# Memory attention: the rests of all key, value and query weights by VectorE, and the query weight sums loaded later

## The chip, the cores and the metric

One core of a Trainium2 chip runs the whole layer. The metric is device time of one execution in microseconds (us). Its engines are TensorE (PE, with its weight loads as PEld), VectorE (DVE), ScalarE (ACT), GpSimd (POOL) and SyncE (SP). SP and POOL issue the DMA transfers of this part; 16 DMA engines of the core carry them.

## The reference

A decoder layer for 512 positions of width 1024: a SwiGLU half-step, token mixing, memory cross-attention, a second SwiGLU half-step, a final norm. The change lies in the cross-attention, which is

```python
def memory_xattn(h, m, w_xq, w_xkv, w_xo):
    q = (h @ w_xq).reshape(B, S, XATTN_HEADS, XATTN_HEAD_DIM) * XATTN_HEAD_DIM ** -0.5
    k, v = jnp.split(m @ w_xkv, 2, axis=-1)
    p = jax.nn.softmax(jnp.einsum('bshd,bmhd->bhsm', q, k).astype(jnp.float32), axis=-1)
    o = jnp.einsum('bhsm,bmhd->bshd', p.astype(v.dtype), v)
    return o.reshape(B, S, D_MODEL) @ w_xo
```

with 256 rows of memory `m`, 4 heads of width 256, and `h` and `m` normed before. Inputs are float32.

## The kernel before

Every float32 operand of a product is kept as two rounded parts: a high part (ScalarE's rounded copy) and the rest (VectorE's `raw - high`). A product is three matmuls: high by high, high by rest, rest by high. `split` (L114, L115) makes the two parts.

The cross-attention first makes keys and values in 16 steps, `for i in range(NKV)`: steps 0 to 7 are the column blocks of the key weights (`in_w_xk_dram`, 24 matmuls of 256 columns each, into `ps_d`), steps 8 to 15 the blocks of the value weights (`in_w_xv_dram`, 12 matmuls of 512 columns each, into two banks `ps_s` for 8 to 11 and two banks `ps_t` for 12 to 15). Each step uses one 512 KB block. It is loaded by SP into one of three buffers `wr` (`fetch`), and `cut` makes its parts: three blocks ahead of the loop, blocks 3 and 4 in step 0, then block i+4 in step i, until block 15 in step 11. So a block is cut four steps before it is used. `cut` ends with the `fetch` of the block that is three further on, which takes the buffer that the cut frees. The parts go into `w` (two halves of 512 columns, blocks in `LOOSE`), `xqh`/`xql` or `wh`/`wl`.

Inside the loop every engine runs its instructions in the order in which the code issues them (`ordered`). In step i come: the cut, the matmuls, the evacuation of the step before (`evacuate`: `kh`, `kl`, and the two `vh`, `vl` behind steps 11 and 15), the calls on query weights, and then one or two pieces of `work`: the normed input as sums of quarters for the query product, made by VectorE with some ScalarE (`yt`, `xph`, `w3h`, `xpl`, `K`, `nh`, `nl`).

For the blocks in `SHARED` the rest isn't made by VectorE. In `added`, ScalarE copies the block twice, once as it is and once negated, and a POOL transfer adds the block from HBM once more to the negated copy.

The query product of a head uses sums of weight blocks, in `xs` (`s` in the code, two buffers): `load_q` has SP load one block twice, `add_q` has POOL add two other halves to it by an adding transfer. `load_r` and `load_r2` load the blocks `r1` (in a `wr` buffer) and `r2`. In steps 12 and 13 the parts of head 0's weights `w1` and `w2` are made. Then `heads(0)` to `heads(3)` follow: `heads(hd)` makes head hd's query in seven products, and in it the sums and parts of head hd+1's weights (`e["s"]`, `e["w1"]`, `e["w2"]`).

Of the kernel before, what the change touches and what calls it, by code (L numbers as in the profile page):

```python
# [71 lines left out]
def hybrid_layer(ctx: ExitStack, tc: tile.TileContext, a: dict):  # L72
# [16 lines left out]
    @contextmanager  # L89
    def ordered():  # L90
        Engine.pinned = True
        yield
        Engine.pinned = False
# [19 lines left out]
    def split(h, l, src):  # L113
        A.activation(h, src, AF.Copy)  # L114
        V.tensor_sub(l, src, f32(h))  # L115

    def wpair():
        return (g.tile([P, 1024], F32R, tag="wh", name="wh", bufs=2),
                g.tile([P, 1024], F32R, tag="wl", name="wl", bufs=2))
# [811 lines left out]
    with tc.tile_pool(name="mix", bufs=1, reuse_waits="tile") as mp:  # L931
# [121 lines left out]
        for c in range(4):  # L1053
            h, l = wload(a["vcat"][:, c * 2 * VC:(c + 1) * 2 * VC], 2 * VC)
            for kk in range(2):
                k = 2 * c + kk
                w = slice(kk * VC, (kk + 1) * VC)
# [385 lines left out]
    with tc.tile_pool(name="xa", bufs=1, reuse_waits="tile") as xp:  # L1443
# [11 lines left out]
        def part(hl, src, j):  # L1455
            split(*hl, src[:, j * 512:j * 512 + 512])
# [4 lines left out]
        kv = [a["w_xk"][m] for m in range(KT)] + [a["w_xv"][f, c] for f in range(2) for c in range(4)]  # L1461
        NKV = len(kv)
        raws, cuts = [], []
        SHARED = (7, 9, 11, 13)
        LOOSE = (0, 1, 2, 7, 8, 9, 12, 13, 14)

        def fetch():
# [5 lines left out]
        def share(i, h, l, c):  # L1473
            if i not in SHARED:
                return split(h, l, raws[i][:, c])
            added(h, l, raws[i][:, c], kv[i][:, c])

        def added(h, l, raw, src):

            A.activation(h, raw, AF.Copy)  # L1480
            A.activation(l, raw, AF.Copy, scale=-1.0)
            G.dma_start(l, src, accum_op=ALU.add)

        def cut():
            i = len(cuts)
            if i in LOOSE:
                cuts.append([[big(F32R, "w0") for _ in range(2)] for _ in range(2)])
                for j in range(2):
                    share(i, cuts[i][0][j], cuts[i][1][j], slice(j * S, j * S + S))
            else:  # L1490
                cuts.append(wpair() if i in (5, 6) else qpair())
                share(i, *cuts[i], slice(0, 1024))
            fetch()
# [6 lines left out]
        def memory(i):  # L1500
            h, l = cuts[i]
            if i < KT:
                pk[i] = bank("d")
                for k in range(KT):
                    for z, (w, m) in enumerate(((h, gh[k]), (h, gl[k]), (l, gh[k]))):
                        w = w[k // 4][:, k % 4 * P:][:, :P] if i in LOOSE else w[:, k * P:(k + 1) * P]
                        T.matmul(pk[i][:, :MEM], w, m, start=k + z == 0, stop=k == KT - 1 and z == 2)
                return
            c = i % 4
            pk[i] = [bank("st"[i // 4 - 2]) for _ in range(MT)] if c == 0 else pk[i - 1]  # L1510
            for kk in range(2):
                k = 2 * c + kk
                w = slice(kk * 512, kk * 512 + 512)
                for t in range(MT):
                    tk = slice(t * P, (t + 1) * P)
                    for z, (m, ww) in enumerate(((gh, h), (gh, l), (gl, h))):
                        T.matmul(pk[i][t], m[k][:, tk], ww[kk] if i in LOOSE else ww[:, w], start=k + z == 0,
                                 stop=k == KT - 1 and z == 2)

        def evacuate(i):  # L1520
            if i < KT:
                split(kh[i], kl[i], pk[i][:, :MEM])
            elif i % 4 == 3:
                for t in range(MT):
                    split(vh[t][i // 4 - 2], vl[t][i // 4 - 2], pk[i][t])
# [3 lines left out]
        def load_q(hd):  # L1529
            w1 = a["w_xq"][2 * hd + 1]  # L1530
            xw[hd]["s"] = xp.tile([P, 1536], F32, tag="S", name="xs3", bufs=2)
            t = xw[hd]["s"][:, 512:].rearrange("p (j c) -> p j c", j=2)
            SY.dma_start(t, bass.AP(w1.tensor, w1.offset, [[1024, P], [0, 2], [1, 512]]))

        def add_q(hd):
            w0 = a["w_xq"][2 * hd]
            t = xw[hd]["s"][:, 512:].rearrange("p (j c) -> p j c", j=2)
            G.dma_start(t, bass.AP(w0.tensor, w0.offset, [[1024, P], [P * 1024 + 512, 2], [1, 512]]),
                        accum_op=ALU.add)

        def load_r(hd):
            xw[hd]["r1"] = raw_tile()
            SY.dma_start(xw[hd]["r1"], a["w_xq"][2 * hd])

        def load_r2(hd):
            d = xw[hd]
            d["r2"] = xp.tile([P, 1024], F32, tag="R2", name="r2", bufs=1)
            SY.dma_start(d["r2"][:, :512], a["w_xq"][2 * hd + 1][:, 512:])
# [55 lines left out]
        with ordered():  # L1604
            for i in range(NKV):
                for _ in range(1 if i else 2):
                    if len(cuts) < NKV:
                        cut()
                    elif len(cuts) == NKV and "r1" not in xw[0]:
                        load_r(0)  # L1610
                        load_r2(0)
                        load_r(1)
                        load_r(2)
                memory(i)
                if i == 0:
                    st = n3.sums()
                    n3.r = n3.rstd(st, NT)
                elif i == 1:
                    n3.spread()
                if i:  # L1620
                    evacuate(i - 1)
                if i in (0, 2):
                    load_q(i // 2)
                elif i in (3, 5):
                    add_q(i // 5)
                if i == NKV - 4:
                    d = xw[0]
                    d["w2"], w = wpair(), wpair()
                    d["w1"] = [[t[:, c:c + 512] for t in w] for c in (0, 512)]
                    added(*w, d["r1"], a["w_xq"][0])  # L1630
                    part([t[:, 512:] for t in d["w2"]], d["s"], 1)
                elif i == NKV - 3:
                    V.tensor_add(d["s"][:, :512], d["s"][:, 1024:], d["r1"][:, :512])
                    part([t[:, :512] for t in d["w2"]], d["s"], 0)
                for _ in range(0 if i < 2 else 1 if i < 9 else 2):
                    if work:
                        work.pop(0)()
            while work:
                work.pop(0)()
            evacuate(NKV - 1)  # L1640
# [274 lines left out]
```

## Time and profile before

| what | us |
|---|---|
| median of 3 runs (lowest, highest) | 1245.64 (1244.54, 1246.74) |
| profiled execution | 1245.68 |
| its span, first to last instruction | 1243.9 |
| PE busy | 1226.9 (99%) |
| DVE busy | 992.9 (80%) |
| ACT busy | 754.0 (61%) |
| POOL busy | 97.3 (8%) |

The span starts at 0; all times below count from there. A matmul that overlaps the next is counted as busy to its modelled end, so 99% doesn't mean that PE runs at its best pace: a wait shows as idle time before an instruction, a low clock as a longer distance from one matmul's start to the next. The granted clock is 1.00 at full speed. The DMA share is the busy share of the 16 engines; it can come out a little over 1.

### The profile page before, as it was taken

The numbers are of one execution on the slowest core, as the hardware profiler recorded it, in microseconds if no ns is written. First come the engines' busy times: TensorE is split into PE (matmuls) and PEld (weight loads), VectorE is DVE, ScalarE is ACT, GpSimd is POOL, SyncE is SP. The second block draws the span as 40 slices with busy tenths as digits, with TensorE's granted clock in tenths as the row PEclk, the third lists the DMA queues.
The fourth block names the chain that finished last, engine by engine and source line by source line (L and its number), as shares of the span: only waits on it lengthen the run. The fifth ranks groups of instructions, "written<-read, shape, count | busy, mean of one in ns | idle before, by whom it ended". The sixth has DMA issues, their size and how long they took to land.

```text
span 1243.9 us, 19322 instructions
## 1 busy us (share of the span) xinstructions
PE 1226.9 (99%) x7113; PEld 1070.2 (86%) x7113; DVE 992.9 (80%) x2018; ACT 754.0 (61%) x1506; POOL 97.3 (8%) x123
## 2 busy tenths in 40 slices
PE   9999999999999999999999997999999999999997
PEld 7888888879989788888887896997888888888997
DVE  5899888888787978787778667775698888889774
ACT  5466666556555777776874456664456666655553
POOL 0001110221110000000001011000001111100000
PEclk9999999999999999999999999999999999999999
DMA  6737775688544522222234377332456777727441
GB/s 223 186 109 194 187 190 149 188 254 246 138 150 129 168 67 84 81 67 77 68 102 169 102 230 202 102 94 68 111 152 169 188 184 196 178 87 207 134 134 69
DMA packets 64944, 181.38 MB, mean 146 GB/s; under 512 B 6616, under 2 KB 6896, under 8 KB 64848
## 3 DMA queue, kind: packets, MB, share of 16 engines
q1 hardware_dynamic: 45920, 132.70, 32.4%
q0 software_dynamic: 18496, 46.63, 18.3%
q8 instruction: 56, 0.92, 0.3%
q10 hardware_dynamic: 432, 0.81, 0.2%
q14 instruction: 40, 0.33, 0.1%
HBM read 175.87 MB, written 10.07 MB: 149 GB/s over the span
## 4 chain that ended last, share of the span: by engine, by line
PE 92%; DVE 3%; DMA 2%; ACT 1%; issue 1%; DVEq 0%; SPq 0%; POOL 0%; ACTq 0%; POOLq 0%
PE ps_d L139 30%; PE ps_d L87 21%; PE ps_t L87 13%; PE ps_s L87 7%; PE ps_o L87 6%; PE ps_d L1313 4%; PE ps_d L614 2%; PE ps_t L1198 1%; PE ps_s L1111 1%; PE ps_o L1106 1%; PE ps_s L1110 1%; PE ps_o L1105 1%; DMA xql<-in_w_xv_dram 1%; DMA xs<-in_w_xq_dram 1%; PE ps_d L1061 1%
## 5 line engine op out<-in xcount | busy, mean ns | idle before, releaser
L114 ACT ACTIVATE wh<-wr 128x512 fp32r<-128x512 f32 (+2 forms) x158 | 105.0, 695 | 100.7 <-issue 44.6
L139 PE MATMUL ps_d<-xh,wl 128*128 128x512 f32 x360 | 144.6, 402 | 0.1
L139 PE MATMUL ps_d<-xh,wh 128*128 128x512 f32 x360 | 143.3, 398 | 0.0
L139 PE MATMUL ps_d<-xl,wh 128*128 128x512 f32 x360 | 143.2, 398 | 0.0
L115 DVE TENSOR_TENSOR wl<-wr,wh 128x512 fp32r<-128x512 f32 (+2 forms) x158 | 119.0, 775 | 22.7 <-ACT wh L114 20.7
L87 DVE TENSOR_TENSOR wl<-wr,wh 128x1024 fp32r<-128x1024 f32 (+2 forms) x73 | 76.9, 1058 | 25.9 <-ACT wh L87 25.7
L139 PEld LDWEIGHTS ps_d<-xh,wl 128*128 128x128 f32 x360 | 67.8, 188 | 13.8 <-DVE wl L115 0.5
L139 PEld LDWEIGHTS ps_d<-xl,wh 128*128 128x128 f32 x360 | 67.8, 188 | 13.1
L87 ACT ACTIVATE wh<-wr 128x1024 fp32r<-128x1024 f32 (+2 forms) x74 | 67.9, 923 | 18.3 <-PE ps_o L87 4.6
L139 PEld LDWEIGHTS ps_d<-xh,wh 128*128 128x128 f32 x360 | 67.9, 189 | 12.9
L87 PE MATMUL ps_d<-b,wh 128*128 128x512 f32 (+1 forms) x220 | 64.0, 350 | 0.0
L87 DVE TENSOR_TENSOR s<-s,wr 128x512 f32<-128x512 f32 (+1 forms) x84 | 63.9, 760 | 0.0
L87 DVE TENSOR_TENSOR h2l<-s,h2h 128x512 fp32r<-128x512 f32 x68 | 44.1, 688 | 8.4 <-ACT h2h L87 8.1
L87 PE MATMUL ps_o<-t,h2h 128*128 128x256 f32 x272 | 50.4, 283 | 0.0
L87 PE MATMUL ps_d<-n,h2h 128*128 128x512 f32 x136 | 49.9, 401 | 0.1
L87 PE MATMUL ps_d<-b,wl 128*128 128x256 f32 x178 | 49.9, 280 | 0.0
L87 PE MATMUL ps_d<-t,h4h 128*128 128x512 f32 x136 | 49.6, 399 | 0.0
L87 PE MATMUL ps_t<-b,h5h 128*128 128x512 f32 x136 | 49.4, 397 | 0.0
L87 PE MATMUL ps_t<-n,h3h 128*128 128x512 f32 x136 | 49.3, 395 | 0.0
L87 PE MATMUL ps_s<-b,wh 128*128 128x512 f32 x136 | 49.1, 395 | 0.0
L1093 ACT ACTIVATE pth<-ps_t 128x512 fp32r<-128x512 f32 (+1 forms) x64 | 32.6, 524 | 18.7 <-PE ps_t L1198 15.5
L87 ACT ACTIVATE h2h<-s 128x512 fp32r<-128x512 f32 x68 | 39.1, 623 | 7.6 <-DVE s L87 7.6
(567 smaller groups left out, 3906.5 us busy)
## 6 DMA issues: line engine op xcount, KB each, us to landing
wr<-in_w_in_dram SPq DMA_DIRECT2D x29, 512.0 KB, 3.6
wr<-in_w_gate_dram SPq DMA_DIRECT2D x25, 512.0 KB, 5.1
wr<-in_w_up_dram SPq DMA_DIRECT2D x25, 512.0 KB, 5.3
wr<-in_w_down_dram SPq DMA_DIRECT2D x24, 448.0 KB, 3.5
s<-in_w_gate_dram SPq DMA_DIRECT2D x17, 512.0 KB, 4.5
s<-in_w_gate_dram POOLq DMA_DIRECT2D x17, 512.0 KB, 6.0
s<-in_w_up_dram SPq DMA_DIRECT2D x17, 512.0 KB, 4.3
s<-in_w_up_dram POOLq DMA_DIRECT2D x17, 512.0 KB, 6.4
```

Source lines behind the costliest of these rows:

```text
L87: return lambda *args, **kw: tc.keep_in_program_order(call(*args, **kw))
L114: A.activation(h, src, AF.Copy)
L115: V.tensor_sub(l, src, f32(h))
L139: yield T.matmul(out, w[:, c], m, start=i == 0, stop=i == total - 1)
L614: T.matmul(two[m], w[:, cc], v, start=f == 0 and z == 0, stop=f == NA - 1 and z == 2)
L1061: T.matmul(pv[i][:, :VC], m[k][:, tk], ww[:, w], start=k == 0 and z == 0, stop=k == KT - 1 and z == 2)
L1093: A.activation(h[:, :n], pt[:, :n], AF.Copy)
L1105: T.matmul(po[:, cols], w, h[:, src], start=start, stop=False, skip_group_check=True)
L1106: T.matmul(po[:, cols], w, l[:, src], start=False, stop=False, skip_group_check=True)
L1110: first = T.matmul(out, q[:, tk], kk[0][:, ks], start=True, stop=False)
L1111: T.matmul(out, q[:, tk], kk[1][:, ks], start=False, stop=True)
L1313: yield T.matmul(pj, w[:, c], m, start=n == 0, stop=n == 11)
```

## The change

`SHARED` becomes empty, so that all 16 blocks are split by ScalarE and VectorE, and the same holds for head 0's `w1`, whose two halves are split in steps 12 and 14. `load_q` of heads 0 and 1 moves from steps 0 and 2 to steps 6 and 12, `add_q` from steps 3 and 5 to steps 8 and 14.

```diff
-        SHARED = (7, 9, 11, 13)
+        SHARED = ()
...
-                if i in (0, 2):
-                    load_q(i // 2)
-                elif i in (3, 5):
-                    add_q(i // 5)
+                if i in (6, 12):
+                    load_q(i // 12)
+                elif i in (8, 14):
+                    add_q(i // 14)
                 if i == NKV - 4:
...
-                    added(*w, d["r1"], a["w_xq"][0])
+                    part(d["w1"][0], d["r1"], 0)
                     part([t[:, 512:] for t in d["w2"]], d["s"], 1)
+                elif i == NKV - 2:
+                    part(d["w1"][1], d["r1"], 1)
                 elif i == NKV - 3:
```

On POOL eight adding transfers go (two halves each for blocks 7, 9 and 13, one whole for block 11, one whole for head 0's `w1`); only the four of the query sums are left. On ACT the negated copies go.

VectorE in step 3, where block 7 is cut (`w` its parts, `wr` the raw block; the rows around it are the first `work` and the rest of the keys of step 2):

```order
 L87 SCALAR_TENSOR_TENSOR xph<-x_7583,gains,rb 128x512
+L87 TENSOR_TENSOR w_8152<-wr,w_8150 128x512
+L87 TENSOR_TENSOR w_8153<-wr,w_8151 128x512
 L87 TENSOR_TENSOR kl<-ps_d,kh 128x256
 L87 TENSOR_TENSOR w3h<-yt 128x256
```

Two subtractions stand now ahead of the evacuation and of the work of that step; blocks 9, 11 and 13 get theirs in the same way (11 as one of 1024 columns).

VectorE from step 12 on (`xs_8073` and `xs_8311` are the sums of head 0, `wl` the rests of its weights, `nl` and `vl` rests of sums of the input and of values):

```order
 L87 TENSOR_TENSOR vl<-ps_s,vh 128x512 x2
-L87 TENSOR_TENSOR wl<-xs_8073,wh 128x512
+L87 TENSOR_TENSOR wl<-wr,wh 128x512
+L87 TENSOR_TENSOR wl<-xs_8311,wh 128x512
 L87 TENSOR_TENSOR nl<-xpl,nh 128x512 x2
-L87 TENSOR_TENSOR xs_8073<-xs_8073,wr 128x512
-L87 TENSOR_TENSOR wl<-xs_8073,wh 128x512
+L87 TENSOR_TENSOR xs_8311<-xs_8311,wr 128x512
+L87 TENSOR_TENSOR wl<-xs_8311,wh 128x512
 L87 TENSOR_TENSOR nl<-w3l,nh 128x512
```

One subtraction for `w1` is new here, and one more stands two rows further down, behind the first rest `nl<-xph`.

SP from the loads of the last key blocks on (`xs_8073` and `xs_8148` are the sums of heads 0 and 1 before, `xs_8311` and `xs_8506` the same now):

```order
 L87 DMA wr<-in_w_xk_dram 128x1024 x2
-L87 DMA xs_8073<-in_w_xq_dram 128x2x512
+L87 DMA wr<-in_w_xv_dram 128x1024 x6
+L87 DMA xs_8311<-in_w_xq_dram 128x2x512
 L87 DMA wr<-in_w_xv_dram 128x1024 x2
-L87 DMA xs_8148<-in_w_xq_dram 128x2x512
-L87 DMA wr<-in_w_xv_dram 128x1024 x6
 L87 DMA wr<-in_w_xq_dram 128x1024
```

The load for head 0 moved behind six value blocks. The load for head 1, not in this piece, stands now behind all value blocks and behind the three loads of `r1`.

## Rows read from the trace of the kernel before

**Rows 1.** Busy us (and instructions) per engine, clock, DMA share, GB/s by stretch:

```profile
core 0: us, PE busy (x) PEld busy (x) DVE busy (x) ACT busy (x) POOL busy (x), PEclk, DMA share, GB/s
721.30:745.91 24.61, 24.61 (x209) 24.61 (x208) 15.69 (x29) 14.58 (x27) 5.88 (x6) 1.00 0.80 227
745.91:765.75 19.84, 13.48 (x51) 9.93 (x50) 16.15 (x33) 11.36 (x20) 2.60 (x3) 0.91 1.06 286
765.75:776.74 10.99, 10.99 (x49) 9.01 (x48) 7.23 (x12) 7.78 (x13) 0.84 (x1) 1.00 0.34 68
```

**Rows 2.** PE in order of time: start, us, what, [idle before <- releaser]:

```profile
750.71 0.50 PE L87 MATMUL ps_s<-w,gh 128*128 128x512 f32 x1 [1.66 <-DMA w<-in_w_xv_dram]
...
753.32 0.50 PE L87 MATMUL ps_s<-w,gh 128*128 128x512 f32 x1 [0.95 <-DMA w<-in_w_xv_dram]
...
761.52 0.50 PE L87 MATMUL ps_s<-xql,gh 128*128 128x512 f32 x1 [3.74 <-DMA xql<-in_w_xv_dram]
...
763.25 0.63 PE L87 MATMUL ps_s<-xqh,gh 128*128 128x512 f32 x1
763.68 0.63 PE L87 MATMUL ps_s<-xql,gh 128*128 128x512 f32 x1
...
786.73 1.59 PE L87 MATMUL ps_d<-K,w 128*128 128x256 f32 x12
```

**Rows 3.** The chain that ended last, 715 to 800: start, us, what:

```profile
732.50 9.04 DMA xs<-in_w_xq_dram
...
749.29 12.19 DMA xql<-in_w_xv_dram
```

**Rows 4.** DMA issues from 738 to 745: KB each, median us to landing:

```profile
w<-in_w_xv_dram POOLq DMA_DIRECT2D x2, 256.0 KB, 11.9
...
xs<-in_w_xq_dram POOLq DMA_DIRECT2D x1, 512.0 KB, 16.4
```

**Rows 5.** DMA issues of the whole execution:

```profile
wr<-in_w_out_dram SPq DMA_DIRECT2D x8, 512.0 KB, 3.6
wr<-in_w_xk_dram SPq DMA_DIRECT2D x8, 512.0 KB, 3.8
wr<-in_w_xv_dram SPq DMA_DIRECT2D x8, 512.0 KB, 7.8
...
xs<-in_w_xq_dram SPq DMA_DIRECT2D x4, 512.0 KB, 5.2
...
wl<-in_w_xq_dram POOLq DMA_DIRECT2D x1, 512.0 KB, 5.3
```

**Rows 6.** DVE in order of time:

```profile
732.34 0.74 DVE L87 SCALAR_TENSOR_TENSOR yt<-x,gains,rb 128x512 f32<-128x512 f32 x1
733.00 0.74 DVE L87 SCALAR_TENSOR_TENSOR xph<-x,gains,rb 128x512 f32<-128x512 f32 x1
733.84 0.42 DVE L87 TENSOR_TENSOR kl<-ps_d,kh 128x256 fp32r<-128x256 f32 x1
734.18 0.41 DVE L87 TENSOR_TENSOR w3h<-yt 128x256 f32<-128x256 f32 x1
...
735.98 1.29 DVE L87 TENSOR_TENSOR w<-wr,w 128x512 fp32r<-128x512 f32 x2
737.18 0.42 DVE L87 TENSOR_TENSOR kl<-ps_d,kh 128x256 fp32r<-128x256 f32 x1
...
782.60 1.23 DVE L87 TENSOR_TENSOR wl<-r,wh 128x1024 fp32r<-128x1024 f32 x1 [2.00 <-ACT wh L87]
...
784.42 0.68 DVE L87 TENSOR_TENSOR xs<-xs,wr 128x512 f32<-128x512 f32 x1
785.02 0.68 DVE L87 TENSOR_TENSOR w<-wr,w 128x512 fp32r<-128x512 f32 x1
```

**Rows 7.** DVE from 721 to 777 by shape: busy us, mean ns, idle before:

```profile
L87 DVE TENSOR_TENSOR kl<-ps_d,kh 128x256 fp32r<-128x256 f32 x8 | 3.4, 421 | 4.2 <-ACT kh L87 4.1
```

**Rows 8.** ACT from 721 to 777 by shape:

```profile
L87 ACT ACTIVATE wh<-wr 128x1024 fp32r<-128x1024 f32 x3 | 3.2, 1051 | 0.0
```

## The prediction

> **What bounds the kernel now.** The shares of busy time come first: PE is busy nearly all the time, so whatever an edit gains has to come out of PE's own waits. The chain that ended last, followed through the cross-attention, leaves PE in one place only for long: it goes through two transfers, the load of a query sum (9.04 us) and the adding transfer of value block 11 (12.19 us) [rows 3]. PE in order of time shows what the chain costs there: three waits in steps 9 and 11, of 1.66, 0.95 and 3.74 us, 6.35 us together, each for an added rest, and behind the longest one matmuls that start 0.43 us apart [rows 2]. The same kind of matmul in steps 12 to 15 needs 10.99 us for 48, so 0.229 us each, at a granted clock of 1.00 [rows 1]. 0.43 us is about twice that, which is the 1.2 GHz level instead of 2.4, after an idle time of PE.
>
> The table by stretch gives the whole loss without counting single matmuls. Steps 8 to 11 and steps 12 to 15 have the same 48 matmuls of 512 columns. The first four take 19.84 us, the last four 10.99 us [rows 1]. The loss is 19.84 - 10.99 = 8.85 us: 6.35 us of idle time and 2.50 us of low clock. In the first stretch the DMA share is 1.06 at 286 GB/s, in the last it is 0.34 [rows 1]; steps 0 to 7 ran at 1.00 clock without a PE wait, but with a DMA share of 0.80 already. So the bound of steps 8 to 11 is transfers. What waits are the adds, 9 to 16 us from issue to landing there [rows 3, 4], while the last add, issued when the engines had little else to do, landed in 5.3 us [rows 5].
>
> **What is removed.** Between steps 3 and 11 four blocks, 4 x 512 KB, are no longer fetched a second time, and these fetches were the only ones for which PE waited. The two query sums (2 x 2 transfers of 512 KB) leave the start of the loop. Left are the plain loads, 512 KB per step, and in the middle the sum of head 0. A step needs 2.75 us of PE (10.99 / 4), so the plain stream is 524 KB / 2.75 us = 191 GB/s, an estimate that leaves a third of the 286 GB/s seen free. Loads at such a pace landed in 3.6 us (the output weights of the stage before) and 3.8 us (key weights) [rows 5]. The three waits go for certain, since no matmul reads an added rest any more; what may be late instead is the subtraction that replaces it. With no wait in place of these the gain is the whole 8.85 us. ScalarE loses its negated copies and is far from full (11.36 of 19.84 us [rows 1]); I cost that at nothing.
>
> **What is added, on VectorE.** A rest of 1024 columns in two halves takes 1.20 us from start to start (735.98 to 737.18), a key rest 0.34 us (733.84 to 734.18), the two scalings of one `work` 1.32 us (2 x 0.66, from 732.34 and 733.00 on, so through at 733.66), the five sums 1.80 us (734.18 to 735.98) [rows 6]; 512 columns are half of 1.20, 0.60 us. Four more blocks are 4.8 us, the two halves of `w1` 1.2 us: 6.0 us more work in the loop. Is there room? I lay VectorE's instructions out in their new order from 733.66 us on, where the trace of before stops to hold: 9 blocks (7 to 15) 10.80, 6 key rests 2.04, 3 scalings 3.96, 4 groups of sums 7.20, 12 rests of input sums 7.20, 2 value rests 1.20, 4 halves of head 0's weights 2.40, one addition 0.60, and one wait of about 0.6 for ScalarE in step 13, where the high part of the sum just made has to come first. That is 36.0 us, so VectorE would be through at 769.7. PE, without waits from 745.91 on, ends step 15 at 745.91 + 96 x 0.229 = 767.9. VectorE is thus full from step 3 on, and behind at the end.
>
> It does no harm as long as each piece is in time. By this layout block 13 is cut at 751.5 and used from 759.6, block 15 at 759.5 and used from 765.1: the cuts are 5 to 8 us early, since a block is cut four steps ahead. At the end head 0's query needs the rest of `r2` (`wl`), in its sixth product. Before, it was done at 783.83, 7.1 us after PE left step 15 at 776.74, and had waited 2.00 us for ScalarE, which hung on PE [rows 6]. Now it would come 1.2 (value rests) + 0.6 (`w3`) + 0.6 (addition) + 1.05 (ScalarE's high part [rows 8]) + 1.23 = 4.7 us behind 769.7, at 774.4, and is needed 7.1 us behind 767.9, at 775.0. So 0.6 us are to spare: the change costs nothing on VectorE by this sum, but hardly more than half a microsecond of further waiting is covered, and beyond that each microsecond is one of the kernel's.
>
> **The loads behind it.** A raw buffer of the four blocks is now free after VectorE's subtraction, not after ScalarE's copy. Block 10's load is issued when block 7 is cut, at 734.9, lands with 3.8 us at 738.7 and is wanted on VectorE at 742.0; the later ones have about the same room. Bounds: 3.6 us landing costs nothing; 7.8 us (the value blocks before [rows 5]) plus 1.05 plus 1.2 for the cut make 10 us for three blocks, 3.3 us each against 2.75 for PE, which over blocks 10 to 15 is 3.3 us of lag, 2.7 of it uncovered at the end. I take nothing, because the 7.8 us were measured at the DMA share of 1.06 that goes.
>
> **The sums moved.** Head 0's load follows block 13's on SP, at 743.2 when block 10 is cut; with 5.2 us [rows 5] it lands at 748.4, and the add in 5.3 to 16.4 us [rows 4, 5], at 753.7 to 764.8. It is wanted at 762.5. POOL has nothing else in its queue then. Head 1's load stands on SP behind the third `r1`, which waits for block 15's buffer, 759.5: load to 764.7, add to 770.0 with 5.3 us. Before it was wanted at 784.42 [rows 6], 7.7 us after step 15; now at 775.6. Both are in time with 5 us and more at the short price, which I take since these transfers fall where the DMA share was 0.34; the long price is a rival below. The query loads that leave steps 0 to 2 gain nothing by themselves: PE had no wait there.
>
> The Trainium skill, DMA: Bandwidth & Descriptors, section Rules for kernel authors, says that a transfer should be issued early and waited for late, so that its fixed cost lies under compute; this speaks against moving the sums. Here the add of head 1 that was issued early took 16.4 us among others [rows 4], so the trace does not bear it out in this stretch; by the rule the late sum would be what PE waits for, 1246.4 us by the last rival.
>
> **The sum.** Profiled execution 1245.68 (0.04 above the median) - 8.85 = 1236.83. I add 0.6 us for a VectorE that has no slack left: **1237.4 us**, own range 1236.3 to 1238.6.
>
> **Rivals.**
> *VectorE becomes the bound.* For: it is laid out without a pause for 36 us. Before it waited 4.1 us in this part for ScalarE's key parts alone [rows 7]. If as much came back, 4.1 - 0.6 = 3.5 us would be lost: 1240.3. Against: most of those waits came when ScalarE itself waited for transfers, or when VectorE was ahead.
> *The plain loads stay slow.* If the loads still need 7.8 us, 2.7 us are lost: 1239.5. For: three buffers only, freed later. Against: 191 GB/s is less than what was moved before.
> *Head 1's sum comes late* (the other side). Its place is VectorE's addition in `heads(0)`, behind which the parts of head 1's weights are queued; PE takes them up at 786.73, 1.7 us after that part started and 1.0 after its 0.68 us were over [rows 2, 6], so from 776.6 on (775.6 + 1.0) PE waits. With a load of 7.8 us and an add of 16.4 us it lands at 759.5 + 24.2 = 783.7; PE loses 7.1 us and some 2.5 us of clock: 1246.4. If VectorE also lags 4.1 us, block 15's buffer is free that much later: 1250.5. It is slower than before from a landing at 783.0 on, and by 0.2% from 785.5. Against: nothing else is on the DMA engines then but the `r1` loads.
> That the change doesn't do what it says can be ruled out: the order shows no add on POOL but the four sums.
>
> **How the numbers follow.** What a measurement can tell from no change is 0.2%, 2.5 us. Forecast 0.62, VectorE as bound 0.18, slow loads 0.08, late sum of head 1 0.12, of which 0.05 beyond 785.5 and 0.07 within 2.5 us of before. So faster 0.88, same 0.07, slower 0.05. The range for 8 in 10 reaches from 1235.7 (the whole gain, and a run as far below as the lowest of before is below its median, 1.1 us) to 1241.5, over the first two rivals.
>
> **What would show it.** Right: no PE wait from 745 to 768 us, the 48 matmuls of steps 8 to 11 in about 11 us at a clock of 1.00; adds of the sums landing in 5 to 7 us, value loads in 4 to 5; DVE over 90% busy from 735 to 768. Wrong: PE waiting for a `w` or `xql` made by VectorE, a gap before the sixth product of head 0 (VectorE late) or before head 1's first (sum late), or a clock below 1.00 in these stretches.

## The result and the profile after

| | before | after |
|---|---|---|
| median of 4 runs each, us | 1245.87 | 1236.53 |
| lowest and highest, us | 1244.54, 1246.74 | 1235.99, 1236.75 |
| ratio after to before | | 0.9925, 95% interval 0.9908 to 0.9943 |
| profiled execution and its span, us | 1245.68, 1243.9 | 1236.75, 1235.0 |
| DVE, ACT, POOL busy, us | 992.9, 754.0, 97.3 | 997.6, 749.5, 90.5 |

The kernel became 9.3 us faster, and its median lies 0.9 us below the 1237.4 that was forecast, a gain of 8.85 us less 0.6. The answer to [rows 1] is the same table over the same three pieces of PE's work, steps 0 to 7, 8 to 11 and 12 to 15 (this execution is 0.7 us later when it comes there):

```profile
core 0: us, PE busy (x) PEld busy (x) DVE busy (x) ACT busy (x) POOL busy (x), PEclk, DMA share, GB/s
722.00:746.61 24.61, 24.61 (x210) 24.61 (x209) 21.11 (x40) 15.53 (x28) 0.00 (x0) 1.00 0.54 179
746.61:757.68 11.07, 11.07 (x51) 9.01 (x50) 11.04 (x22) 5.11 (x10) 1.23 (x1) 1.00 0.90 264
757.68:768.68 11.00, 11.00 (x50) 9.01 (x49) 10.27 (x19) 7.53 (x16) 1.20 (x1) 1.00 0.53 158
```

Steps 8 to 11 take 11.07 us where they took 19.84, and the other two stretches are as long as before: the whole gain stands in one row. PE is busy throughout at a clock of 1.00. VectorE is busy 11.04 of 11.07 us there, and 97% of the time from 735 to 768 us: it has hardly any idle time left. The 16 steps as a whole went from 55.44 to 46.68 us, 8.76 us less; the 0.7 us by which the part ahead of them was longer and the 0.8 us by which the part behind was shorter in this execution I did not follow.

In the chain that ended last no transfer is left in this place (start, us, what); the two rows of [rows 3] have no successor:

```profile
722.15 2.86 PE ps_d L87 x24
...
746.77 11.07 PE ps_s L87 x48
757.84 11.00 PE ps_t L87 x48
768.84 1.43 PE ps_d L87 x12
```

VectorE in order of time, the rows that answer to [rows 6]:

```profile
734.36 1.29 DVE L87 TENSOR_TENSOR w<-wr,w 128x512 fp32r<-128x512 f32 x2
...
758.83 1.22 DVE L87 TENSOR_TENSOR xql<-wr,xqh 128x1024 fp32r<-128x1024 f32 x1
...
770.37 1.28 DVE L87 TENSOR_TENSOR vl<-ps_t,vh 128x512 fp32r<-128x512 f32 x2
...
774.53 1.23 DVE L87 TENSOR_TENSOR wl<-r,wh 128x1024 fp32r<-128x1024 f32 x1 [1.68 <-ACT wh L87]
...
776.36 0.68 DVE L87 TENSOR_TENSOR xs<-xs,wr 128x512 f32<-128x512 f32 x1
```

From the first row, block 7's rest, to the third, which follows the last of the loop's work, it is 770.37 - 734.36 = 36.0 us, as laid out. The transfers of the whole execution (KB each, median us to landing), against [rows 5]:

```profile
wr<-in_w_xk_dram SPq DMA_DIRECT2D x8, 512.0 KB, 3.7
wr<-in_w_xv_dram SPq DMA_DIRECT2D x8, 512.0 KB, 4.4
xs<-in_w_xq_dram SPq DMA_DIRECT2D x4, 512.0 KB, 4.0
xs<-in_w_xq_dram POOLq DMA_DIRECT2D x4, 512.0 KB, 5.9
```

The value loads went from 7.8 to 4.4 us, and the adds of the sums that had 16.4 us in [rows 4] to 5.9 in the median (6.0 for head 0, 7.0 for head 1).

### The profile page after: what moved, and what is told of

Read it like the earlier page. It is cut to its first block, busy times and chain, and to the rows that moved or that the text cites. A ratio compares the mean times of both kernels' runs of the same rounds, so it can differ in the third digit from the quotient of the medians.

```text
span 1235.0 us, 19306 instructions
## 1 busy us (share of the span) xinstructions
PE 1225.8 (99%) x7113; PEld 1069.5 (87%) x7113; DVE 997.6 (81%) x2027; ACT 749.5 (61%) x1499; POOL 90.5 (7%) x115
## 4 chain that ended last, share of the span: by engine, by line
PE 95%; DVE 3%; ACT 1%; DMA 1%; issue 0%; DVEq 0%; SPq 0%; ACTq 0%
PE ps_d L139 31%; PE ps_d L87 22%; PE ps_t L87 13%; PE ps_s L87 8%; PE ps_o L87 6%; PE ps_d L1313 4%; PE ps_d L614 2%; PE ps_t L1198 1%; PE ps_s L1111 1%; PE ps_o L1106 1%; PE ps_s L1110 1%; PE ps_o L1105 1%; PE ps_d L1061 1%; DVE F L971 1%; PE ps_t L1278 0%; PE ps_s L987 0%
## 5 line engine op out<-in xcount | busy, mean ns | idle before, releaser
L87 PEld LDWEIGHTS ps_d<-b,wh 128*128 128x128 f32 x220 | 38.6, 188 | 6.0
```

Of the source, the lines that this page charges most:

```text
L87: return lambda *args, **kw: tc.keep_in_program_order(call(*args, **kw))
```

## The experiments

All are edits of the changed kernel. Each ratio is to the kernel before on the same chip, so they compare with 0.9925 (0.9908 to 0.9943).

**One part of the change at a time.** First without the move of the query sums:

```diff
-                if i in (6, 12):
-                    load_q(i // 12)
-                elif i in (8, 14):
-                    add_q(i // 14)
+                if i in (0, 2):
+                    load_q(i // 2)
+                elif i in (3, 5):
+                    add_q(i // 5)
```

> The changed kernel with the loads of the query sums back at steps 0 and 2 and their adds at steps 3 and 5; all rests by VectorE. Theory A (the transfers of steps 3 to 11 are too many; PE waited for added rests only): without added rests nothing waits for an add, the plain loads get slower than 4.4 us but have room, so about 1237 us and PE without a wait in steps 8 to 11. Theory B (an add in itself is too slow, whatever else moves): 1236.5 us as well. Theory C (the early sums alone made the loss): the loss stays, 1243 to 1246 us, with PE waiting for rests that wait for loads of 7 to 8 us.

The ratio is 0.9926 (0.9912 to 0.9941), the median 1237.52 us. Nearly the whole gain is there without the move, and theory C falls; A and B forecast the same here. One wait appears on PE, ahead of head 0's third product:

```profile
771.76 0.51 PE L87 MATMUL ps_d<-K,wh 128*128 128x256 f32 x2 [0.85 <-ACT ps_d L87]
```

Then only the move (and `w1` by VectorE), with the four blocks by adds again:

```diff
-        SHARED = ()
+        SHARED = (7, 9, 11, 13)
```

> Blocks 7, 9, 11 and 13 again by adding transfers, the query sums late as in the changed kernel, w1 of head 0 by VectorE. Theory A (contention): with the early sums gone the adds of the blocks land in 6 to 8 us instead of 10 to 12, which is inside the 9 us that a block has from its copies to its use, so most of the gain is there: 1236.5 to 1239 us. Theory B (adds too slow in themselves): landing stays at 9 to 12 us, PE waits as before, 1243 to 1246 us. Theory C (only the early sums made the loss): 1236.5 us.

The ratio is 0.9952 (0.9937 to 0.9967), the median 1240.66 us, between A and B. The landing of 6 to 8 us that A needs did not come. The adds of blocks 7 and 9 took 8.7 to 10.3 us, although no query sum was under way when they were issued; that of block 11 took 8.5 us, and those of block 13, beside the add of head 0's sum, 12.0 us. What came earlier is the issue: the plain loads landed in 6.9 us instead of 7.8, and the add of block 11 was issued at 746.46 us instead of 749.29. So PE waits less, and later:

```profile
754.99 0.50 PE L87 MATMUL ps_s<-xql,gh 128*128 128x512 f32 x1 [0.44 <-DMA xql<-in_w_xv_dram]
762.90 0.50 PE L87 MATMUL ps_t<-w,gh 128*128 128x512 f32 x1 [2.11 <-DMA w<-in_w_xv_dram]
764.87 0.50 PE L87 MATMUL ps_t<-w,gh 128*128 128x512 f32 x1 [0.32 <-DMA w<-in_w_xv_dram]
```

2.87 us of waits stand where 6.35 us stood, and all are for adds. So the rests by VectorE alone bring the whole gain within the noise, the later sums alone about two thirds of it, and the two halves of the change overlap.

And the add for head 0's `w1` put back:

```diff
-                    part(d["w1"][0], d["r1"], 0)
+                    added(*w, d["r1"], a["w_xq"][0])
...
-                elif i == NKV - 2:
-                    part(d["w1"][1], d["r1"], 1)
```

> The changed kernel with the rest of head 0's w1 by an adding transfer again, as before the change. PE has no wait from step 0 to the end of head 0 in the changed kernel, so the 1.2 us that VectorE is spared can win nothing, and the add has landed in time before (5.3 us): 1236.5 us within 1. A rival, that this last add is late as the others were once it stands beside the late query sums, says 1238 us or more, with PE waiting for wl ahead of head 0's first product.

The ratio is 0.9913 (0.9899 to 0.9928), the median 1236.22 us, and PE has no wait from step 0 to head 1: this part of the change neither costs nor gains anything measurable. (The profiled execution is the slowest of the four, 1238.55 us; it reaches step 0 1.8 us later than that of the changed kernel, so the difference lies ahead of this part.)

**How much VectorE has left.** Subtractions are made twice:

```diff
             split(h, l, v)
+            if n1 == "n2":
+                V.tensor_sub(l, v, f32(h))
```

> The changed kernel with four subtractions of 512 columns on VectorE done twice (the second rests of the input sums, steps 11 to 13), 2.4 us of work more. The sum in the prediction says that VectorE has some 0.6 to 0.9 us left at head 0's sixth product and that beyond it each us costs one: 1236.5 + 1.5 = 1238.0 us, PE waiting ahead of that product for a rest by VectorE. The rival, that VectorE is off the path with its cuts 5 to 8 us early, says 1236.5 us.

The ratio is 0.9941 (0.9925 to 0.9958), the median 1238.48 us. By the intervals alone that is not told apart from the changed kernel; the waits on PE tell it:

```profile
771.97 0.50 PE L87 MATMUL ps_d<-K,wh 128*128 128x256 f32 x2 [1.01 <-ACT ps_d L87]
...
777.44 0.38 PE L87 MATMUL ps_d<-K,wl 128*128 128x256 f32 x1 [0.29 <-DVE wl L87]
```

With `n1 in ("n2", "b21")` it is eight:

> As the run with four subtractions done twice, but eight (steps 11 to 15), 4.8 us of work more. By the sum 4.8 - 0.9 = 3.9 us are lost, and up to 2.5 us more if the clock falls behind the wait: 1240.4 to 1243 us. VectorE off the path: 1236.5 us.

The ratio is 0.9963 (0.9950 to 0.9976), the median 1241.68 us. PE has four waits, 4.04 us together:

```profile
772.42 0.50 PE L87 MATMUL ps_d<-K,wh 128*128 128x256 f32 x2 [1.00 <-ACT ps_d L87]
...
776.02 0.39 PE L87 MATMUL ps_d<-nl,wh 128*128 128x256 f32 x1 [0.70 <-DVE nl L87]
...
778.57 1.70 PE L87 MATMUL ps_d<-K,w 128*128 128x256 f32 x12 [2.05 <-ACT ps_d L87]
...
780.80 0.39 PE L87 MATMUL ps_d<-K,wl 128*128 128x256 f32 x1 [0.29 <-DVE wl L87]
```

4.8 us of work cost about 4.7 us by the ratios: VectorE is next to the bound, as the sum said. The place is another than the sum had. The first wait stands ahead of the third product, and ScalarE is named, not VectorE. That product adds on to a bank that ScalarE copies first, and ScalarE gets to the copy late because it waits in step 13 for VectorE's addition. In the changed kernel that wait is 3.47 us, here it is 5.65 us:

```profile
765.49 0.63 ACT L87 ACTIVATE wh<-xs 128x512 fp32r<-128x512 f32 x1 [3.47 <-DVE xs L87]
...
767.37 0.63 ACT L87 ACTIVATE wh<-xs 128x512 fp32r<-128x512 f32 x1 [5.65 <-DVE xs L87]
```

**The price of a late sum.**

```diff
-                if i in (6, 12):
-                    load_q(i // 12)
-                elif i in (8, 14):
-                    add_q(i // 14)
+                if i == 6:
+                    load_q(0)
+                elif i == 8:
+                    add_q(0)
...
             if hd < 3:
                 load_r2(hd + 1)
+            if hd == 0:
+                load_q(1)
+                add_q(1)
```

> The changed kernel with the load and the add of head 1's query sum issued inside head 0, behind the load of r2 (776 us instead of 760). Load 4 us and add 6 us put the landing at about 786 us, VectorE wants it at 776.4, PE is covered for 1.0 us more: PE waits some 8.5 us ahead of head 1's first product and loses up to 2.5 us of clock: 1245 to 1248 us. Were that sum not on the path: 1236.5 us.

The ratio is 1.0003 (0.9994 to 1.0013), the median 1247.34 us: the whole gain is gone. VectorE waited for the sum, PE for VectorE:

```profile
785.36 0.69 DVE L87 TENSOR_TENSOR xs<-xs,wr 128x512 f32<-128x512 f32 x1 [10.16 <-DMA xs<-in_w_xq_dram]
```

```profile
786.71 2.51 PE L87 MATMUL ps_d<-K,w 128*128 128x256 f32 x10 [8.90 <-DVE w L87]
```

The granted clock from 786 to 800 us, behind the wait, was 0.85, so the wait of 8.90 us is followed by a slow stretch, as the one of 3.74 us was before [rows 2] (0.60 from 761.52 to 765.75).

**The load without anyone waiting for it.** Four copies of 512 KB into HBM, issued by POOL at the cuts where the adds stood. In the first form the source was the block in HBM:

```diff
             fetch()
...
+            if i in (7, 9, 11, 13):
+                G.dma_start(spare[i // 2 - 3], kv[i])
```

> The changed kernel with four more transfers, issued by POOL behind the cuts of blocks 7, 9, 11 and 13: each copies the block of 512 KB to a spare place in HBM, and nothing waits for them. They put load on the DMA engines where the adds stood. Theory A (what counts is that a matmul waits for an add; plain loads have room): 1236.5 to 1237.5 us. Theory D (the load alone slows the plain loads until VectorE, which has nothing to spare, lags): 1238 to 1240 us with value loads at 6 us or more.

The ratio is 0.9910 (0.9893 to 0.9926), the median 1235.98 us, but the run does not test what it should. A copy from HBM waits for nothing, and POOL issued three of the four before the loop:

```profile
659.87 0.52 POOL L87 DMA_DIRECT2D spare<-in_w_xk_dram  x1
660.38 0.98 POOL L87 DMA_DIRECT2D spare<-in_w_xv_dram  x2
750.03 1.26 POOL L87 DMA_DIRECT2D xs<-in_w_xq_dram  x1 [88.66 <-ACT K L87]
750.80 1.01 POOL L87 DMA_DIRECT2D spare<-in_w_xv_dram  x1
```

The same with the query sums at steps 0, 2, 3 and 5:

> The same four copies, and the query sums at steps 0, 2, 3 and 5 as before the change: as many bytes at the same places as before, but no matmul waits for an added rest. Theory A: 1237 to 1238 us. Theory D: value loads at 7 to 8 us, VectorE lags, 1239.5 us and more.

The ratio is 0.9938 (0.9923 to 0.9953), the median 1239.76 us. Here POOL's queue held three copies back behind the adds of the sums, to 734 and 740 us, and value loads took 6.1 us. That fits theory D, but with the copies bunched. So the copies were paced: they read the high parts from SBUF and so wait for ScalarE, as the adds did.

```diff
+            if i in (7, 9, 11, 13):
+                hs = cuts[i][0]
+                if i in LOOSE:
+                    for j in range(2):
+                        G.dma_start(spare[i // 2 - 3][:, j * S:j * S + S], f32(hs[j]))
+                else:
+                    G.dma_start(spare[i // 2 - 3], f32(hs))
```

> The changed kernel with four copies of 512 KB by POOL, of the high parts of blocks 7, 9, 11 and 13 to a spare place in HBM, each waiting for ScalarE as the adds did (the copies of the two runs before this one waited for nothing and were issued early). Nothing waits for them but the reuse of a tile. Query sums late. The load of the adds without anyone waiting for them: value loads at 5 to 6 us, VectorE lags by a part of a microsecond: 1236.5 to 1238.5 us. If the load alone made the loss: 1242 us or more.

The ratio is 0.9922 (0.9907 to 0.9936), the median 1236.90 us; value loads take 4.7 us and PE has no wait in the loop: the DMA engines had room for that much.

> The same four copies with the query sums at steps 0, 2, 3 and 5: the transfers of the kernel before at the places of before, with all rests by VectorE. The loss of before then splits: what remains here is the price of the load (plain loads late, VectorE lagging), the rest was PE waiting for adds. From the run with early copies (1239.8) 1239 to 1242 us, with PE waiting once, ahead of head 0's third product. Only awaited adds cost: 1237.5 us. Load alone: 1244 us or more.

The ratio is 0.9946 (0.9929 to 0.9962), the median 1239.41 us. This kernel has the transfers of before in number, size and place, but for head 0's `w1`, with copies where the adds of the four blocks stood. The DMA share is nearly back (0.97 from 728 to 746 us, 1.03 from 746.6 to 757.7, where it was 0.99 and 1.09), value loads take 6.3 us, and still PE has no wait in steps 8 to 15. It has one behind them, and the stretch with it has a clock of 0.85 (PE's wait; then the stretches, columns as above):

```profile
772.64 0.51 PE L87 MATMUL ps_d<-K,wh 128*128 128x256 f32 x2 [1.77 <-ACT ps_d L87]
```

```profile
746.60:757.70 11.10, 11.10 (x50) 9.04 (x49) 10.60 (x21) 6.41 (x12) 1.66 (x3) 1.00 1.03 333
...
768.70:780.00 11.30, 9.53 (x68) 9.32 (x67) 9.17 (x16) 7.56 (x16) 0.00 (x0) 0.85 0.08 23
```

The gain splits by it, if the steps are taken in this order. (1 - 0.9946) of 1246 us are 6.7 us, gained as soon as no matmul waits for an add while nearly as much moves; the other 9.3 - 6.7 = 2.6 us come when that load goes too. They are paid through late loads, a late VectorE (it waits 2.32 us for block 10's high part and 0.43 us for block 11's, which ScalarE makes late because their loads are late) and a late copy of ScalarE. Both intervals are some 2 us wide to each side and they overlap, so the split is one of about two thirds to one third and no finer, and the ratios alone would not tell the smaller part from nothing. What tells it is the wait in the trace, and the run with the paced copies and late sums on the same chip: all its times (1236.04 to 1237.03 us) lie below all of this one (1238.76 to 1241.27 us). Since the copies load the DMA engines a little less than the adds did, 2.6 us is rather too little for the load.

## Why the prediction was right

**The removed waits.** 19.84 - 10.99 = 8.85 us was read as the whole gain; 8.77 us came in those steps (19.84 to 11.07). It held because the same matmuls stood in the same profile once with and once without the waits, so that the low clock behind a wait was in the difference too, without a model of it. One link the prediction left out: the add of block 11 did not only land late, it was issued late. ScalarE has to make both copies of the block first, and the block's load took 9.6 us; now it takes 3.9 us, and the first copy starts 4 us earlier (before, then after):

```profile
746.99 1.06 ACT L87 ACTIVATE xqh<-wr 128x1024 fp32r<-128x1024 f32 x1 [1.13 <-DMA wr<-in_w_xv_dram]
...
742.96 1.06 ACT L87 ACTIVATE xqh<-wr 128x1024 fp32r<-128x1024 f32 x1 [0.39 <-DMA wr<-in_w_xv_dram]
```

**VectorE's layout.** 36.0 us were summed from pitches (start to start, not durations) and 36.0 us measured. The 6.0 us more on VectorE fit, because blocks are cut four steps early and it had one wait only, in step 13 for ScalarE, 0.70 us where 0.6 was laid out. The rival that its waits for ScalarE's key parts come back did not come true; of 4.1 us in [rows 7] 1.1 us are left:

```profile
L87 DVE TENSOR_TENSOR kl<-ps_d,kh 128x256 fp32r<-128x256 f32 x8 | 3.3, 418 | 1.1 <-ACT kh L87 1.1
```

**Where VectorE would show.** Here the step was off, without harm to the number: head 0's sixth product was named as the first place, with 0.6 us to spare. `wl` was ready at 775.76 for a matmul at 776.05, but it had waited for ScalarE, and ScalarE for PE, as before: VectorE itself stood idle for 1.68 us ahead of it. The tight place is the third product, through ScalarE's copy, which ends at 770.68 (0.37 us from 770.31 on) for a matmul at 771.55:

```profile
770.31 0.37 ACT L87 ACTIVATE ps_d<-ps_d 128x256 f32<-128x256 f32 x1
```

0.9 us are to spare there. The 0.6 us that the forecast added for a full VectorE were not paid; that is the distance from 1237.4 to the 1236.75 of the profiled execution. That VectorE's new work stayed within these 0.9 us was partly luck: the prediction costed ScalarE at nothing and did not look at this copy.

**The plain loads.** 4.4 us landing, near the 3.8 taken and far from 7.8. The rival that they stay slow was priced at 2.7 us; with as many transfers as before and nobody waiting for adds it came to 2.6 us by the ratios, through a lag on VectorE as it said. That the sizes agree so well is luck: the 2.7 us were lag alone, and what was measured is a wait of 1.77 us at another place and the low clock behind it.

**The sums moved.** Head 0's add landed at 750.43 + 6.0 = 756.4 for a copy by ScalarE at 760.34, head 1's at 765.55 + 7.0 = 772.6 for an addition at 776.36: in time by 3.9 and 3.8 us, where the prediction had 5 us and more, since it took 5.3 us for an add. The rule that a transfer should be issued early (the Trainium skill, DMA: Bandwidth & Descriptors, section Rules for kernel authors) did not decide. With no adds for the blocks, early or late makes no measurable difference (0.9926 against 0.9925); with the paced copies beside them the early sums were the slower ones, 1239.41 us against 1236.90 on the same chip. Later than in the changed kernel the rule holds, near the price forecast for the last rival: some 15 us more, and all is lost. That the query loads which leave steps 0 to 2 "gain nothing by themselves" was too flat: with the adds kept, the move alone (with `w1`, which made no measurable difference) brought 0.9952, since it takes load from transfers that PE waits for.

## What to carry to other kernels

Where one stretch of a profile repeats the same instructions with and without waits, the difference of the two lengths is the gain to expect, clock included, as long as nothing else comes to bind. Before work is moved from a transfer to an engine, lay out that engine's instructions in the new order by their pitch and look for the first thing that waits for it, also by way of another engine that waits for it in its own queue. A transfer that makes part of an operand has to be judged by its landing time beside all others that are under way, not by its time alone.

## What was not expected of the hardware

An adding transfer of 512 KB landed in 5.3 to 7.0 us at DMA shares up to 0.90, but adding transfers of 256 and 512 KB took 8.5 to 16.4 us at shares of 0.88 to 1.09, with value loads of 7.8 us in the median beside them before and of 4.4 us without the blocks' adds. Two of the runs set an add beside a copy: the one with the late sums only and the one with paced copies and late sums have the same 3.67 MB on POOL's queue from 722 to 800 us, as adds in the first and as copies to HBM in the second, at nearly the same times. From 728 to 746 us (columns as above, the run with adds first):

```profile
728.00:746.00 18.00, 18.00 (x154) 18.00 (x153) 13.35 (x26) 12.56 (x24) 3.43 (x4) 1.00 0.88 239
...
728.00:746.00 18.00, 18.00 (x154) 18.00 (x153) 16.27 (x31) 11.76 (x23) 2.70 (x5) 1.00 0.80 257
```

The adds keep the engines busier and fewer bytes are moved. Those of blocks 7 and 9 land in 9.5 and 9.0 us in the median, the copies in 5.1 and 4.7 us, and the value loads take 6.9 us beside the adds, 4.7 us beside the copies. So an add takes more of the engines than such a copy per byte counted; that a plain load from HBM stands as the copy does was not measured.

A wait of PE did not always cost clock as well. Behind waits of 2.11 us (late sums only) and 2.05 us (eight more subtractions) the granted clock stayed at 1.00; behind the 1.77 us of the last run it was 0.58 from 772.6 to 776.3 us. What makes the difference is open.
